# Two decoder layers: two weight blocks of a following stage split ahead into large buffers, and no weight remainders on GpSimd beside a norm

## The chip, the core and the metric

One core of a Trainium2 chip runs the whole program. The metric is device time of one execution in microseconds. A kernel's time is the median of its runs; the profile is one further execution, recorded instruction by instruction. PE is TensorE, DVE VectorE, ACT ScalarE, POOL GpSimd, and SP the engine that issues nearly all of the DMAs.

## The reference

512 tokens of width 1024 pass two layers. Layer 0 mixes tokens with multi-head latent attention, layer 1 with a sparse attention whose indexer picks keys per token. Each layer then cross-attends with 4 heads into 256 memory tokens and applies a SwiGLU FFN of hidden width 2816. Every sub-layer ends in a scaled residual and a layer norm:

```python
for i in range(DEPTH):
    y = mla_mixer(...) if i % 2 == 0 else dsa_mixer(...)
    x = layer_norm(ALPHA * x + y, ln_g[i, 0], ln_b[i, 0])
    y = memory_cross_attention(x, mem, xa_w_q[i], xa_w_kv[i], xa_w_o[i])
    x = layer_norm(ALPHA * x + y, ln_g[i, 1], ln_b[i, 1])
    y = swiglu_ffn(x, ffn_w_in[i], ffn_w_down[i])
    x = layer_norm(ALPHA * x + y, ln_g[i, 2], ln_b[i, 2])
```

## The kernel before

Everything is fp32, but TensorE multiplies in a rounded form (fp32r). So each operand is split into a high part, a cast on ACT (L103), and a low part, the remainder, a subtraction on DVE or, where the caller asks for it, on POOL (L105). A product is three matmuls, high by high, high by low, low by high (`mm3`, L126 to L129).

Weights come in blocks of 128x1024 (512 KB). `chunk` (L114) loads one with a DMA on SP's queue into `raw`, of which there are three buffers, and splits it into `wh` and `wl`, five buffers each. Activations live in a pool of 9 larger buffers (`t8`, 8 KB per partition): the residual stream x (2), its transposed split copies XT (4), a norm's coefficients gb (1), and the down-projection weights of the FFN with their sums and differences (`sp_weights`). A scheduler puts each engine's instructions in order by the program's order and by what they wait for, and gives each tile a buffer that is free; each engine then works through its list strictly in order.

The end of a sub-layer works on four tiles tt of 128 tokens. `out_proj_tm` (L407) multiplies the tokens of a tile with the output weights in two halves n of 512 columns, four k steps each. DVE adds each half to the residual (L367) and takes its statistics (L316). `Norm.affine` then merges the statistics (L324), adds the epsilon (L286), takes the power -1/2 on POOL, on one column (L288), and normalizes each half in two operations on DVE (L343, L345). `Norm.turn` transposes the eight 128x128 squares of the normalized tile on PE (L355) and splits them into XT, a cast from PSUM on ACT and a remainder on DVE. These steps are interleaved: affine(tt-1) comes behind the first half of tile tt, turn(tt-2) behind its k=1. The first tile ran k-major: for each k both halves n. So its n=0 was finished as the seventh of eight products.

Behind the second norm of each layer comes the first FFN group (`ffn`). It needs the four blocks (jj, gu) = (0,0), (0,1), (1,0), (1,1) of `ffn_in`; a pair gu = 0, 1 is a gate and its linear partner. Their products are taken in halves of 256 tokens, first all four blocks for tokens 0 to 255, with turn(2) and turn(3) of the norm behind the products of the first and the third, then all four for tokens 256 to 511. The blocks with jj + gu = 1 had their remainders on POOL.

Behind the third norm of layer 0 the sparse-attention layer begins with the value/indexer weights w_vi, 328 columns by 8 k steps, in three blocks of k 0 to 3, 3 to 6 and 6 to 8. The remainder of the middle one was on POOL. The products of token tile tt need all three blocks.

In cross-attention (`cross`), the query blocks of head hd+1 are loaded and multiplied while head hd is at work; then come that head's two key blocks `xa_k`. Head 3's queries are the last reader of XT in `cross`.

Of the kernel before, what the change touches and what calls it, by code (L numbers as in the profile page):

```python
# [11 lines left out]
F32 = mybir.dt.float32  # L12
# [8 lines left out]
P = 128  # L21
# [48 lines left out]
def tile_hybrid_mla_dsa_deepnorm_block(ctx: ExitStack, tc: tile.TileContext, A: dict, out: bass.AP):  # L70
# [42 lines left out]
    def chunk(src, shape, eng=None, after=(None, None)):  # L113
        n = int(np.prod(shape[1:]))  # L114
        raw = wp.tile([P, 1024], F32, tag="raw", name=nm("raw"), bufs=3)
        with behind(after[0]):
            load[0] = nc.sync.dma_start(raw[:, :n], src)
        h = wp.tile([P, 1024], FR, tag="wh", name=nm("wh"))
        l = wp.tile([P, 1024], FR, tag="wl", name=nm("wl"))
        split(h[:, :n], l[:, :n], raw[:, :n], eng, after[1])  # L120
        if len(shape) == 2:
            return h[:, :n], l[:, :n]
        k = shape[1]
        return (h[:, :n].rearrange("p (k m) -> p k m", k=k), l[:, :n].rearrange("p (k m) -> p k m", k=k))

    def mm3(ps, st, mv, start, stop, more=False):  # L126
        nc.tensor.matmul(ps, st[0], mv[0], start=start, stop=False, skip_group_check=more)  # L127
# [284 lines left out]
    def out_proj_tm(src, w, kc, norm):  # L412

        ws = [[chunk(w(n, c), (P, 2, 512)) for c in range(kc)] for n in range(2)]
        for tt in range(NT):
            ts_ = slice(P * tt, P * tt + P)

            def part(ps, n, k, c0, c1):
                sh, sl = src(k)
                wh, wl = ws[n][k // 2]  # L420
                return mm3(ps[:, c0:c1], (sh[:, ts_], sl[:, ts_]), (wh[:, k % 2, c0:c1], wl[:, k % 2, c0:c1]),
                           k == 0, k == 2 * kc - 1)

            first = [bank("b") for _ in range(2)] if tt == 0 else None
            if first:
                for k in range(2 * kc):
                    for n in range(2):
                        part(first[n], n, k, 0, 512)
            for n in range(2):
                parts = TAIL if n and norm.last and tt == NT - 1 else ((0, 512),)  # L430
                for c0, c1 in parts:
                    ps = first[n] if first else bank("b")
                    for k in range(0 if first else 2 * kc):
                        end = part(ps, n, k, c0, c1)
                        if tt > 1 and n == 0 and k == 1:
                            norm.turn(tt - 2, end)
                    if tt and n == 0:
                        norm.affine(tt - 1)
                    residual(ps, tt, n, False, c0, c1)
                    norm.stat(tt, n, c0, c1)  # L440
        norm.affine(NT - 1)
# [356 lines left out]

    def cross(i, XT, m, kv0):
        OT = []  # L800
        kvs = {0: kv0}
        pairs = []
        steps = iter(())

        def more(n):
            for _ in range(n):
                next(steps, None)

        def q_proj(hd):
            ws = [chunk(A["xa_q"][i, 2 * hd + dt], (P, NK, P)) for dt in range(2)]  # L810
            pq = proj_tiles(ws, XT, hd == 0)
            Q = []
            for dt in range(2):
                q = (t2(FR), t2(FR))
                split(q[0], q[1], pq[dt])
                Q.append(q)
            return Q

        def scores(hd, Q):
            Kt = kvs[hd][0]  # L820
            Sp = [t2(), t2()]
            sx = Softmax([Sp[qt // 2][:, 256 * (qt % 2):256 * (qt % 2) + 256] for qt in range(NT)])
            for qt in range(NT):
                ps = bank("b" if hd < 2 else "a")
                ts_ = slice(P * qt, P * qt + P)
                for dt in range(2):
                    mm3(ps[:, 0:256], (Q[dt][0][:, ts_], Q[dt][1][:, ts_]), (Kt[0][:, dt], Kt[1][:, dt]), dt == 0, dt == 1)
                sx.exp(qt, ps[:, 0:256], 1.0 / 16.0)
            return sx

        def turned(sx):
            Ss = sx.normalise()
            PT = []
            for mb in range(2):
                pt = bank("a")
                for qt in range(NT):
                    nc.tensor.transpose(pt[:, P * qt:P * qt + P], Ss[qt][:, P * mb:P * mb + P], ident)
                p_ = (t2(FR), t2(FR))
                split(p_[0], p_[1], pt)
                PT.append(p_)  # L840
            return PT

        def pv(hd, PT):
            Vt = kvs[hd // 2 * 2][1]
            eo = []
            for dt in range(2):
                po = bank("a")
                ds_ = slice(256 * (hd % 2) + P * dt, 256 * (hd % 2) + P * dt + P)
                for mb in range(2):
                    mm3(po, (Vt[mb][0][:, ds_], Vt[mb][1][:, ds_]), PT[mb], mb == 0, mb == 1)  # L850
                if hd < 2:
                    o = t2()
                    nc.scalar.copy(o, po)
                    eo.append(o)
                else:
                    o = (t2(FR), t2(FR))
                    split(o[0], o[1], po)
                    OT.append(o)
            if hd < 2:
                pairs.append(sp_operands(*eo))  # L860

        Q = q_proj(0)
        for hd in range(4):
            if hd == 1:
                W = sp_weights(A["xa_og"][i])
            Ss = scores(hd, Q)
            if hd < 3:
                more(1)
                Q = q_proj(hd + 1)
                more(2)  # L870
            else:
                more(3)
            PT = turned(Ss)
            if hd < 3:
                more(1)
                kvs[hd + 1] = xa_kv(i, hd + 1, m)
                more(1)
            else:
                more(3)
            pv(hd, PT)  # L880
            if hd == 1:
                steps = sp_steps(pairs, W, set())
                more(1)
            elif hd == 2:
                more(1)
        for _ in steps:
            pass
        return OT

    def sp_operands(e, o):  # L890

# [67 lines left out]
                radd(ps[t], t0 + t, n)  # L959
            yield  # L960

    def ffn(i, prev, norm_of, between=None):
        XT = prev.XT
        touched = set()
        steps = iter(())
# [12 lines left out]
        for gi, (j0, j1) in enumerate(FFN_GROUPS):  # L978
# [8 lines left out]
                WN = sp_weights(A["ffn_dg"][i, gi - 1])  # L987
            for j in range(j0, j1, 2):
                if j == 0:
                    ws = [chunk(A["ffn_in"][i, jj, gu], (P, NK, P), nc.gpsimd if jj + gu == 1 else None)  # L990
                          for jj in (j, j + 1) for gu in range(2)]
                    pss = proj_tiles(ws, XT, True, prev)
                    eo = [gate(pss[2 * jj], pss[2 * jj + 1]) for jj in range(2)]
                else:
                    eo = []
                    for jj in (j, j + 1):
                        pgu = []
                        for gu in range(2):
                            w = chunk(A["ffn_in"][i, jj, gu], (P, NK, P))
                            if first and gu:  # L1000
                                W.update(sp_weights(A["ffn_d0"][i], load[0]))
                                WN = sp_weights(A["ffn_dg"][i, 0])
                                first = False
                            if not first:
                                next(steps, None)
                            ps = bank("a")
                            proj(ps, w, XT, (0, 512))
                            if not first:
                                next(steps, None)
                            pgu.append(ps)  # L1010
                        eo.append(gate(*pgu))
                if not last:
                    pairs.append(sp_operands(*eo))
# [9 lines left out]
    out_proj(lambda k: OTs[k], lambda n, c: A["mla_o"][n, c], 4, norm, True)  # L1023
    mem = load_mem()
    kv0 = xa_kv(0, 0, mem)
    OT = cross(0, norm.XT, mem, kv0)
    norm = Norm(load_ln(0, 1))
    out_proj_tm(lambda k: OT[k], lambda n, c: A["xa_o"][0, n, c], 2, norm)
    norm = ffn(0, norm, lambda: Norm(load_ln(0, 2), spill=True), general_bias())
    r = nc.values_load(flag[0:1, 0:1], engines=(mybir.EngineType.SP,), min_val=0, max_val=1)  # L1030
    XT = norm.XT

# [7 lines left out]
    def stack_q_pool(ps, QA, QB):  # L1040
# [4 lines left out]
        nc.gpsimd.tensor_tensor(QA[64:128], f[0:64], QA[0:64].bitcast(F32), op=ALU.subtract)  # L1045
        nc.gpsimd.tensor_tensor(QB[0:64], f[64:128], QB[64:128].bitcast(F32), op=ALU.subtract)

    wvs = [chunk(A["w_vi"][:, NV * k0:NV * k1], (P, k1 - k0, NV), nc.gpsimd if k0 == 3 else None)
           for k0, k1 in ((0, 3), (3, 6), (6, 8))]
    VD = t8(FR, (P, 4, 4, P))  # L1050
    pk = bank("b")
    wi = cp.tile([P, NT, 8], F32, name="wi")
# [216 lines left out]
    out_proj(lambda k: OTd[k], lambda n, c: A["dsa_o"][n, c], 4, norm, True, pins)  # L1269
    mem = load_mem()  # L1270
    kv0 = xa_kv(1, 0, mem)
    OT = cross(1, norm.XT, mem, kv0)
    norm = Norm(load_ln(1, 1))
    out_proj_tm(lambda k: OT[k], lambda n, c: A["xa_o"][1, n, c], 2, norm)
    ffn(1, norm, lambda: Norm(load_ln(1, 2), last=True))

# [79 lines left out]
```

## Time and profile before

| | |
|---|---|
| median of 3 runs | 1520.51 us (1519.79 to 1521.77) |
| the profiled execution | 1521.89 us |
| its span, first to last instruction | 1520.0 us |
| granted TensorE clock, mean | 0.995 |

The page of the profile gives busy time by engine and a strip of 40 slices; groups of instructions are named by line and engine, with the time of one and the idle time ahead of it; a wait is named by the engine and the line that ended it. A row of a timeline has the start, the duration, the engine, the line, the operation, the output, the inputs and the count of merged instructions; where several are merged or follow without a gap, the durations overlap a little, so the distance of two starts is the better price of one. Stretches of time can be asked for with the busy time of every engine in each and the clock that PE was granted.

### The profile page before, as it was taken

What the parts mean: (1) busy time and instruction counts of PE and PEld (TensorE: products, weight loads), DVE (VectorE), ACT (ScalarE), POOL (GpSimd) and SP (SyncE); (2) the same over time, 40 slices, a digit from 0 to 9 for tenths busy, and PEclk for the clock granted to TensorE, in tenths of its full rate; (3) what the DMA queues carried; (4) which work ended last, traced back from release to release, by engine and by line L of the source; (5) the groups of instructions that cost most, each with busy time, mean ns of one, the idle gap of its engine ahead of it and who ended that gap; (6) DMA issues with size and microseconds to landing.
All of it is one profiled execution on the core that took longest, in us unless ns stands there. A gap on an engine that the chain in (4) does not pass through costs nothing. (4 is left out here: it accounts for less than half of the span.)

```text
span 1520.0 us, 20327 instructions
## 1 busy us (share of the span) xinstructions
PE 1481.5 (97%) x7600; PEld 1259.2 (83%) x7600; DVE 1073.5 (71%) x1818; ACT 670.2 (44%) x1196; POOL 374.9 (25%) x344
## 2 busy tenths in 40 slices
PE   9999999999999999999999989999999999999997
PEld 7788888988888888888888778898888888888886
DVE  7787869667857666565678989685678576566646
ACT  4677753444234333333256588344442433333331
POOL 1322003020223233150024653030103233142302
PEclk9999999999999999999999999999999999999999
DMA  6234423422332323222243146353323234223231
GB/s 216 72 103 111 149 82 128 154 82 83 99 110 98 125 71 125 90 95 93 91 153 102 53 161 227 111 167 98 104 77 111 70 99 137 85 96 125 71 97 56
DMA packets 50280, 166.16 MB, mean 109 GB/s; under 512 B 5188, under 2 KB 11732, under 8 KB 47364
## 3 DMA queue, kind: packets, MB, share of 16 engines
q1 hardware_dynamic: 49604, 163.61, 32.9%
q8 instruction: 60, 0.98, 0.3%
q10 hardware_dynamic: 576, 1.25, 0.2%
q14 instruction: 40, 0.33, 0.1%
HBM read 160.60 MB, written 9.47 MB: 112 GB/s over the span
## 5 line engine op out<-in xcount | busy, mean ns | idle before, releaser
L127 PE MATMUL ps<-t,wh 128*128 128x512 f32 (+2 forms) x1248 | 452.7, 363 | 6.0 <-DVE t L105 3.4
L128 PE MATMUL ps<-t,wh 128*128 128x512 f32 (+2 forms) x1248 | 450.5, 361 | 1.2 <-DVE t L105 1.2
L129 PE MATMUL ps<-t,wl 128*128 128x512 f32 (+2 forms) x1248 | 450.7, 361 | 0.0
L103 ACT CAST wh<-raw 128x1024 fp32r<-128x1024 f32 (+2 forms) x205 | 213.8, 1043 | 335.3 <-PE ps L128 148.3
L105 DVE TENSOR_TENSOR wl<-raw,wh 128x1024 fp32r<-128x1024 f32 (+3 forms) x179 | 246.6, 1380 | 123.1 <-ACT wh L103 122.1
L127 PE MATMUL ps<-wh,t 128*128 128x512 f32 (+3 forms) x760 | 289.5, 381 | 0.6 <-ACT wh L103 0.6
L128 PE MATMUL ps<-wl,t 128*128 128x512 f32 (+3 forms) x760 | 288.0, 379 | 1.9 <-DVE wl L105 1.9
L129 PE MATMUL ps<-wh,t 128*128 128x512 f32 (+3 forms) x760 | 287.7, 379 | 0.5 <-DVE t L105 0.4
L127 PEld LDWEIGHTS ps<-t,wh 128*128 128x128 f32 x1248 | 236.0, 189 | 44.0 <-DVE t L105 5.5
L128 PEld LDWEIGHTS ps<-t,wh 128*128 128x128 f32 x1248 | 236.2, 189 | 36.0 <-DVE t L105 1.5
L129 PEld LDWEIGHTS ps<-t,wl 128*128 128x128 f32 x1248 | 236.1, 189 | 35.1
L103 ACT CAST t<-ps 128x512 fp32r<-128x512 f32 (+2 forms) x241 | 118.2, 523 | 126.1 <-PE ps L355 86.7
L103 ACT CAST wh<-t 128x1024 fp32r<-128x1024 f32 (+1 forms) x84 | 82.3, 980 | 204.4 <-PE ps L128 172.2
L128 PEld LDWEIGHTS ps<-wl,t 128*128 128x128 f32 x760 | 143.6, 189 | 27.1 <-DVE wl L105 2.4
L129 PEld LDWEIGHTS ps<-wh,t 128*128 128x128 f32 x760 | 143.4, 189 | 26.5 <-DVE t L105 1.0
L127 PEld LDWEIGHTS ps<-wh,t 128*128 128x128 f32 x760 | 143.5, 189 | 25.4 <-ACT wh L103 0.8
L105 DVE TENSOR_TENSOR wl<-t,wh 128x1024 fp32r<-128x1024 f32 (+1 forms) x84 | 101.5, 1208 | 84.0 <-ACT wh L103 82.5
L105 DVE TENSOR_TENSOR t<-ps,t 128x512 fp32r<-128x512 f32 (+2 forms) x241 | 138.3, 603 | 13.9 <-ACT t L103 11.8
L288 POOL TENSOR_TENSOR sm<-sm,mhalf 128x1 f32<-128x1 f32 x32 | 30.4, 950 | 415.2 <-DVE sm L286 415.2
L105 DVE TENSOR_TENSOR t<-t,t 128x512 fp32r<-128x512 f32 (+3 forms) x133 | 102.8, 778 | 36.7 <-ACT t L103 34.0
L103 ACT CAST t<-t 128x512 fp32r<-128x512 f32 (+3 forms) x133 | 75.3, 572 | 84.9 <-POOL t L899 51.6
L970 DVE TENSOR_TENSOR t<-ps,t 128x512 f32<-128x512 f32 x44 | 30.4, 692 | 108.5 <-PE ps L129 108.5
(182 smaller groups left out, 1767.8 us busy)
## 6 DMA issues: line engine op xcount, KB each, us to landing
raw<-in_ffn_in_dram SPq DMA_DIRECT2D x88, 512.0 KB, 3.5
t<-in_ffn_dg_dram SPq DMA_DIRECT2D x16, 1024.0 KB, 5.1
raw<-in_xa_k_dram SPq DMA_DIRECT2D x16, 512.0 KB, 3.6
raw<-in_xa_v_dram SPq DMA_DIRECT2D x16, 512.0 KB, 4.6
raw<-in_xa_q_dram SPq DMA_DIRECT2D x16, 512.0 KB, 3.6
scr<-vscr SPq DMA_DIRECT2D x16, 319.5 KB, 4.3
raw<-in_w_uq_dram SPq DMA_DIRECT2D x8, 512.0 KB, 3.8
raw<-in_mla_o_dram SPq DMA_DIRECT2D x8, 512.0 KB, 4.2
```

Source lines behind the costliest of these rows:

```text
L103: nc.scalar.copy(h, src)
L105: low[0] = (eng or nc.vector).tensor_tensor(l, src, h.bitcast(F32), op=ALU.subtract)
L127: nc.tensor.matmul(ps, st[0], mv[0], start=start, stop=False, skip_group_check=more)
L128: nc.tensor.matmul(ps, st[0], mv[1], start=False, stop=False, skip_group_check=more)
L129: return nc.tensor.matmul(ps, st[1], mv[0], start=False, stop=stop, skip_group_check=more)
L288: nc.gpsimd.tensor_tensor(b, a, mhalf, op=ALU.pow)
L970: nc.vector.tensor_tensor(sg, pu, sg, op=ALU.mult)
```

## The change

It has three parts.

First, `chunk_ahead`. It loads a block through `raw` like `chunk`, but splits it into one large `t8` buffer, high part and remainder side by side, both on ACT and DVE. In `cross`, behind the queries of head 3, it takes the first two blocks (0,0) and (0,1) of the FFN's input; in the last group of layer 0's FFN, behind the first product of its last gate pair, it takes the first two blocks of w_vi.

Second, the blocks (1,0) and (1,1) and the third one of w_vi, still loaded by `chunk` in their old places, have their remainders on DVE. No remainder in these three places is on POOL any more: two in each FFN, one at w_vi.

Third, the first tile of `out_proj_tm` takes its eight products in another order, so that n=0 is finished as the fifth.

```diff
+    def chunk_ahead(src, k):
+        n = src.shape[-1]
+        raw = wp.tile([P, 1024], F32, tag="raw", name=nm("raw"), bufs=3)
+        nc.sync.dma_start(raw[:, :n], src)
+        t = t8(FR, (P, 2, 1024))
+        h, l = t[:, 0, :n], t[:, 1, :n]
+        split(h, l, raw[:, :n])
+        return [x.rearrange("p (k m) -> p k m", k=k) for x in (h, l)]
...
             if first:
-                for k in range(2 * kc):
-                    for n in range(2):
-                        part(first[n], n, k, 0, 512)
+                for n, k in ((0, 0), (0, 1), (0, 2), (1, 0), (0, 3), (1, 1), (1, 2), (1, 3)):
+                    part(first[n], n, k, 0, 512)
...
                 Q = q_proj(hd + 1)
+                if hd == 2:
+                    ahead += [chunk_ahead(A["ffn_in"][i, 0, gu], NK) for gu in range(2)]
...
                 if j == 0:
-                    ws = [chunk(A["ffn_in"][i, jj, gu], (P, NK, P), nc.gpsimd if jj + gu == 1 else None)
-                          for jj in (j, j + 1) for gu in range(2)]
+                    ws = ahead + [chunk(A["ffn_in"][i, j + 1, gu], (P, NK, P)) for gu in range(2)]
...
                             pgu.append(ps)
+                            if tail and (jj, gu) == (NJ - 1, 0):
+                                ahead += tail()
...
-    norm = ffn(0, norm, lambda: Norm(load_ln(0, 2), spill=True), general_bias())
+    norm = ffn(0, norm, ahead, lambda: Norm(load_ln(0, 2), spill=True), general_bias(),
+               lambda: [chunk_ahead(A["w_vi"][:, NV * k0:NV * k1], k1 - k0) for k0, k1 in ((0, 3), (3, 6))])
...
-    wvs = [chunk(A["w_vi"][:, NV * k0:NV * k1], (P, k1 - k0, NV), nc.gpsimd if k0 == 3 else None)
-           for k0, k1 in ((0, 3), (3, 6), (6, 8))]
+    wvs = ahead[-2:] + [chunk(A["w_vi"][:, 6 * NV:8 * NV], (P, 2, NV))]
```

What this moves, engine by engine; the lines of the changed kernel stand nine to twelve later (L288 is its L297, L316 its L325, L324 its L333, L286 its L295, L343 its L352, L345 its L354, L367 its L376, L923 to L925 its L934 to L936). POOL from the second norm of layer 0 to the first combination of down-projection weights, before; `sm` are the norm's one-column statistics, numbers tell tiles apart:

```order
L288 TENSOR_TENSOR sm_4267<-sm_4265,mhalf 128x1
L288 TENSOR_TENSOR sm_4322<-sm_4320,mhalf 128x1
L105 TENSOR_TENSOR wl_4420<-raw_4417,wh_4419 128x1024
L288 TENSOR_TENSOR sm_4377<-sm_4375,mhalf 128x1
L105 TENSOR_TENSOR wl_4426<-raw_4423,wh_4425 128x1024
L288 TENSOR_TENSOR sm_4405<-sm_4403,mhalf 128x1
L923 TENSOR_TENSOR t_1061_4742<-t_1060_4741 128x512
```

The same place in the changed kernel:

```order
L297 TENSOR_TENSOR sm_4277<-sm_4275,mhalf 128x1
L297 TENSOR_TENSOR sm_4332<-sm_4330,mhalf 128x1
L297 TENSOR_TENSOR sm_4387<-sm_4385,mhalf 128x1
L297 TENSOR_TENSOR sm_4415<-sm_4413,mhalf 128x1
L934 TENSOR_TENSOR t_1059_4740<-t_1058_4739 128x512
```

The two remainders between the powers of tiles 1 to 3 are gone from POOL's list. DVE at the norm of tile 3 in the same window, before; t_659 is the half of x that holds tiles 2 and 3, t_970 the coefficients, and the rows from `ps` are remainders of transposed tiles:

```order
L345 SCALAR_TENSOR_TENSOR t_659_2510<-t_659_2510,sm_4377,t_970_4188 128x512
L316 BN_STATS sm_4384<-t_659_2510 128x6
L367 TENSOR_TENSOR t_659_2510<-t_659_2510,ps_4386 128x512
L105 TENSOR_TENSOR wl_4432<-raw_4429,wh_4431 128x1024
L316 BN_STATS sm_4384<-t_659_2510 128x6
L105 TENSOR_TENSOR t_972_4192<-ps_4463,t_971_4191 128x4x128
L324 BN_AGGR sm_4401<-sm_4384 128x2
L105 TENSOR_TENSOR t_974_4194<-ps_4470,t_973_4193 128x4x128
L286 TENSOR_SCALAR sm_4403<-sm_4401 128x1
L343 SCALAR_TENSOR_TENSOR t_659_2510<-t_659_2510,sm_4401,t_970_4188 128x512 x2
L345 SCALAR_TENSOR_TENSOR t_659_2510<-t_659_2510,sm_4405,t_970_4188 128x512 x2
L105 TENSOR_TENSOR wl_4707<-raw_4704,wh_4706 128x1024
```

In the changed kernel:

```order
L354 SCALAR_TENSOR_TENSOR t_659_2510<-t_659_2510,sm_4387,t_974_4198 128x512
L325 BN_STATS sm_4394<-t_659_2510 128x6
L376 TENSOR_TENSOR t_659_2510<-t_659_2510,ps_4396 128x512
L105 TENSOR_TENSOR wl_4430<-raw_4427,wh_4429 128x1024
L325 BN_STATS sm_4394<-t_659_2510 128x6
L105 TENSOR_TENSOR wl_4705<-raw_4702,wh_4704 128x1024
L333 BN_AGGR sm_4411<-sm_4394 128x2
L105 TENSOR_TENSOR t_976_4202<-ps_4461,t_975_4201 128x4x128
L295 TENSOR_SCALAR sm_4413<-sm_4411 128x1
L352 SCALAR_TENSOR_TENSOR t_659_2510<-t_659_2510,sm_4411,t_974_4198 128x512 x2
L354 SCALAR_TENSOR_TENSOR t_659_2510<-t_659_2510,sm_4415,t_974_4198 128x512 x2
```

The remainder of block (2,0), which stood behind the norm of tile 3 (the last row before), now stands ahead of its L324; one of the two remainders of tile 2's transposes has gone behind the norm. SP's queue at head 3 of the cross-attention, before:

```order
L117 DMA raw_3814<-in_xa_q_dram 128x1024
L117 DMA raw_3926<-in_xa_k_dram 128x1024
L117 DMA raw_3956<-in_xa_k_dram 128x1024
L117 DMA raw_4195<-in_xa_o_dram 128x1024
L117 DMA raw_4201<-in_xa_o_dram 128x1024
```

In the changed kernel, where L129 is the DMA of `chunk_ahead`:

```order
L117 DMA raw_3814<-in_xa_q_dram 128x1024
L129 DMA raw_3878<-in_ffn_in_dram 128x1024
L129 DMA raw_3883<-in_ffn_in_dram 128x1024
L117 DMA raw_3936<-in_xa_k_dram 128x1024
L117 DMA raw_3966<-in_xa_k_dram 128x1024
L117 DMA raw_4205<-in_xa_o_dram 128x1024
```

The two ahead loads stand in front of the key blocks, and hold two of the three staging buffers there.

More of the change, by code (lines that the diff above doesn't have):

```diff
@@ L800, in cross @@
         OT = []
+        ahead = []
         kvs = {0: kv0}
@@ L887, in cross @@
             pass
-        return OT
+        return OT, ahead
     def sp_operands(e, o):
@@ L960, in sp_steps, with ffn @@
             yield
-    def ffn(i, prev, norm_of, between=None):
+    def ffn(i, prev, ahead, norm_of, between=None, tail=None):
         XT = prev.XT
@@ L1025, in tile_hybrid_mla_dsa_deepnorm_block @@
     kv0 = xa_kv(0, 0, mem)
-    OT = cross(0, norm.XT, mem, kv0)
+    OT, ahead = cross(0, norm.XT, mem, kv0)
     norm = Norm(load_ln(0, 1))
     out_proj_tm(lambda k: OT[k], lambda n, c: A["xa_o"][0, n, c], 2, norm)
-    norm = ffn(0, norm, lambda: Norm(load_ln(0, 2), spill=True), general_bias())
+    norm = ffn(0, norm, ahead, lambda: Norm(load_ln(0, 2), spill=True), general_bias(),
+               lambda: [chunk_ahead(A["w_vi"][:, NV * k0:NV * k1], k1 - k0) for k0, k1 in ((0, 3), (3, 6))])
     r = nc.values_load(flag[0:1, 0:1], engines=(mybir.EngineType.SP,), min_val=0, max_val=1)
@@ L1271, in tile_hybrid_mla_dsa_deepnorm_block @@
     kv0 = xa_kv(1, 0, mem)
-    OT = cross(1, norm.XT, mem, kv0)
+    OT, ahead = cross(1, norm.XT, mem, kv0)
     norm = Norm(load_ln(1, 1))
     out_proj_tm(lambda k: OT[k], lambda n, c: A["xa_o"][1, n, c], 2, norm)
-    ffn(1, norm, lambda: Norm(load_ln(1, 2), last=True))
+    ffn(1, norm, ahead, lambda: Norm(load_ln(1, 2), last=True))
 def _fm(w):
```

## The prediction

> **What bounds the kernel now.** I read the page first, then the waits of TensorE, then its rows around the longest of them, then VectorE and GpSimd at the same moments. The page gives TensorE nearly the whole span:
>
> ```profile
> PE 1481.5 (97%) x7600; PEld 1259.2 (83%) x7600; DVE 1073.5 (71%) x1818; ACT 670.2 (44%) x1196; POOL 374.9 (25%) x344
> ```
>
> So time can only be won where TensorE stands still, 1520.0 - 1481.5 = 38.5 us in all, or where it runs at less than its full clock. The table of waits (total, times, longest) puts one reason at the head:
>
> ```profile
> PE ps L355 <- DVE t L345: 6.2, 6, 1.3
> ```
>
> L355 is the transpose of a normalized token tile, L345 the second half of that normalization on VectorE. The six waits are three in each layer, where the second norm (after cross-attention) runs into the first FFN group. TensorE's timeline in the first layer (start, duration, group, in brackets idle time and releaser):
>
> ```profile
> 404.81 1.04 PE L355 MATMUL ps<-ident,t 128*128 128x128 f32 x8
> 405.60 0.47 PE L127 MATMUL ps<-wh,t 128*128 128x512 f32 x1
> ...
> 412.68 0.60 PE L355 MATMUL ps<-ident,t 128*128 128x128 f32 x4
> 414.53 0.63 PE L355 MATMUL ps<-ident,t 128*128 128x128 f32 x4 [1.25 <-DVE t L345]
> ...
> 420.63 0.28 PE L129 MATMUL ps<-t,wl 128*128 128x256 f32 x1
> ...
> 423.80 0.36 PE L127 MATMUL ps<-t,wh 128*128 128x256 f32 x1
> ...
> 425.32 0.28 PE L127 MATMUL ps<-t,wh 128*128 128x256 f32 x1
> ```
>
> The eight transposes of tile 1 run unhindered and cost 405.60 - 404.81 = 0.79 us from start to start. Those of tile 2 break in the middle: 414.53 - 412.68 = 1.85, where half of 0.79 would do, so 1.45 is lost. Between the last product before tile 3's transposes and the first behind them lie 3.17 us; 0.12 (one product's spacing) and 0.79 would do, so 2.26 is lost. Window 1 (about 404 to 425): **3.71 us**.
>
> The second layer has the same window:
>
> ```profile
> 1159.10 0.60 PE L355 MATMUL ps<-ident,t 128*128 128x128 f32 x4
> 1160.99 0.63 PE L355 MATMUL ps<-ident,t 128*128 128x128 f32 x4 [1.29 <-DVE t L345]
> ...
> 1167.10 0.28 PE L129 MATMUL ps<-t,wl 128*128 128x256 f32 x1
> ...
> 1173.27 0.28 PE L127 MATMUL ps<-t,wh 128*128 128x256 f32 x1
> ```
>
> Tile 2 loses 1.89 - 0.40 = 1.49. For tile 3 I compare like with like: 1167.10 and 1173.27 are the same two products as 420.63 and 425.32; here 6.17 us lie between them, there 4.69, so the loss is 2.26 + 1.48 = 3.74. Window 3: **5.23 us**. The extra 1.48 is clock, as the table of stretches shows (length, busy time and count of PE, PEld, DVE, ACT, POOL, then granted clock, DMA share, GB/s):
>
> ```profile
> 386.00:424.00 38.00, 34.93 (x203) 30.33 (x202) 34.48 (x50) 9.06 (x12) 12.84 (x9) 1.00 0.26 86
> 700.00:742.00 42.00, 42.00 (x187) 34.78 (x186) 20.89 (x24) 13.09 (x16) 0.00 (x0) 1.00 0.31 97
> 1168.00:1172.00 4.00, 2.80 (x14) 2.57 (x15) 4.00 (x4) 1.18 (x2) 2.84 (x2) 0.72 0.30 57
> 1172.00:1176.00 4.00, 4.00 (x31) 4.00 (x30) 1.21 (x3) 0.00 (x0) 0.00 (x0) 0.85 0.85 335
> ```
>
> Right behind window 3's stalls the granted clock is 0.72 and 0.85; window 1 stays at 1.00 with the same stalls.
>
> Window 2 is the start of the sparse-attention layer, where the remainder of the third value/indexer weight block comes late:
>
> ```profile
> 770.50 0.41 PE L128 MATMUL ps<-wl,t 128*128 128x328 f32 x1 [1.53 <-DVE wl L105]
> ```
>
> 1.53 idle, and by the ratio of 1.45 lost to 1.25 idle above some 0.2 for the restart: **1.7 us**.
>
> Why VectorE is late: in 386 to 424 it works 34.48 of 38 us, and part of that work is stretched. VectorE and GpSimd, window 1:
>
> ```profile
> 406.36 2.77 DVE L343 SCALAR_TENSOR_TENSOR t<-t,sm,t 128x512 f32<-128x512 f32 x1
> ...
> 410.26 2.20 DVE L345 SCALAR_TENSOR_TENSOR t<-t,sm,t 128x512 f32<-128x512 f32 x1
> ...
> 413.65 0.74 DVE L345 SCALAR_TENSOR_TENSOR t<-t,sm,t 128x512 f32<-128x512 f32 x1
> 414.31 0.68 DVE L316 BATCH_NORM_STATS2 sm<-t 128x6 f32<-128x512 f32 x1
> 414.91 0.66 DVE L367 TENSOR_TENSOR t<-t,ps 128x512 f32<-128x512 f32 x1
> 415.50 1.21 DVE L105 TENSOR_TENSOR wl<-raw,wh 128x1024 fp32r<-128x1024 f32 x1
> 416.64 0.68 DVE L316 BATCH_NORM_STATS2 sm<-t 128x6 f32<-128x512 f32 x1
> 417.24 0.67 DVE L105 TENSOR_TENSOR t<-ps,t 128x512 fp32r<-128x512 f32 x1
> 417.83 0.19 DVE L324 BATCH_NORM_AGGREGATE sm<-sm 128x2 f32<-128x12 f32 x1
> 417.95 0.63 DVE L105 TENSOR_TENSOR t<-ps,t 128x512 fp32r<-128x512 f32 x1
> 418.50 0.13 DVE L286 TENSOR_SCALAR sm<-sm 128x1 f32<-128x1 f32 x1
> 418.56 1.40 DVE L343 SCALAR_TENSOR_TENSOR t<-t,sm,t 128x512 f32<-128x512 f32 x2
> 419.88 3.45 DVE L345 SCALAR_TENSOR_TENSOR t<-t,sm,t 128x512 f32<-128x512 f32 x2
> ```
>
> ```profile
> 406.18 2.41 POOL L105 TENSOR_TENSOR wl<-raw,wh 128x1024 fp32r<-128x1024 f32 x1 [5.45 <-ACT wh L103]
> ...
> 409.52 2.40 POOL L105 TENSOR_TENSOR wl<-raw,wh 128x1024 fp32r<-128x1024 f32 x1
> ...
> 419.68 1.42 POOL L923 TENSOR_TENSOR t<-t 128x512 f32<-128x512 f32 x1
> ```
>
> An affine half costs 0.74 where GpSimd is quiet (0.66 from start to start), but 2.77 and 2.20 beside GpSimd's two weight remainders; each ends about 0.54 behind GpSimd's, as if it had done its work only then: 406.36 + 2.77 = 409.13 against 408.59, and 412.46 against 411.92. Operations that read PSUM (L367, the L105 of t<-ps) show no such thing. The last pair costs 3.45 instead of 1.40 beside the first combination of down-projection weights on GpSimd (L923).
>
> **The change part by part.**
>
> *Remainders off GpSimd, window 1.* The stretched halves return 2.77 - 0.74 = 2.03 and 2.20 - 0.74 = 1.46, 3.49 us ahead of tile 2's last L345. The first tile's new order finishes column half n=0 two products earlier, so its residual add and statistics run while n=1 is still being multiplied. Ahead of L324 stand two L367 and two L316 of 0.6 each: before, all four count from the seventh product, now the last two count from the eighth. A product is three matmuls of 512 columns, an estimated 3 x 0.24 = 0.7 by the 0.12 of 256 columns, so tile 0's L324, and the unbroken list behind it, comes 2.4 - 0.7 - 1.2 = 0.5 to 0.6 earlier. Tile 2 is normalized at 413.65 + 0.66 - 3.49 - 0.6 = 410.2; TensorE asks for its second half at 412.68 + 0.40 = 413.1. The stall of 1.45 goes, with 2.9 us to spare.
>
> *Tile 3.* From 410.2 VectorE does, by the starts in the rows above, L316 0.60, L367 0.59, the remainder of block (1,1) 1.14, L316 0.60, then a remainder that stood behind the norm before (block (2,0), 1.14 more), L324 0.12, one t<-ps remainder 0.6, L286 0.06, L343 1.32 for both halves, L345 0.66 each: 417.7. TensorE comes to the second half of tile 3's transposes at 420.63 + 0.12 - 1.45 + 0.40 = 419.7. Slack 2.0 us, so the 2.26 goes too. The weights that L923 combines arrive later in the changed program (their load waits for the norm's coefficient buffer, which is free only behind this L345), so L923 lands behind the norm, where VectorE has its slack.
>
> *Ahead loads.* Two 1.05 us casts and two 1.2 us remainders per layer move to head 3 of cross-attention. The holes there, on ScalarE and on VectorE, and the load that pays:
>
> ```profile
> 353.96 1.05 ACT L103 CAST wh<-t 128x1024 fp32r<-128x1024 f32 x1 [3.90 <-PE ps L128]
> ```
>
> ```profile
> 346.13 1.22 DVE L105 TENSOR_TENSOR wl<-raw,wh 128x1024 fp32r<-128x1024 f32 x1
> ...
> 355.04 1.23 DVE L105 TENSOR_TENSOR wl<-t,wh 128x1024 fp32r<-128x1024 f32 x1 [3.61 <-ACT wh L103]
> ```
>
> ```profile
> raw<-in_xa_k_dram SPq DMA_DIRECT2D x16, 512.0 KB, 3.6
> ```
>
> ```profile
> 360.46 0.28 PE L127 MATMUL ps<-t,wh 128*128 128x256 f32 x1
> ```
>
> 2.1 of 3.90 and 2.4 of 3.61 us are taken. On SP's queue the two loads go in front of head 3's key blocks, and with three staging buffers the second key block's load now waits for the first one's remainder, which ends at 346.13 + 1.22 = 347.35. It lands 3.6 later near 351.0, is cast by 352.1 and split by 353.3; TensorE wants it at 360.46. Slack 7 us, cost nothing. The ahead tiles take the old activations' buffers, free when head 3's query product is done with them, which is what ScalarE's cast at 353.96 waited for behind its hole (its releaser is TensorE's L128); the loads of the output projection go out some 7 us later, behind the ahead splits, and are wanted only at the out-projection, whose third tile TensorE is at when row 404.81 comes.
>
> *Window 2.* The two early blocks are split in the last FFN group (row 700:742: TensorE full, VectorE busy 20.89 of 42, ScalarE 13.09), which adds 2.3 and 2.1 us there, covered. The affine half there that ran beside the middle block's remainder on GpSimd:
>
> ```profile
> 762.08 2.65 DVE L343 SCALAR_TENSOR_TENSOR t<-t,sm,t 128x512 f32<-128x512 f32 x1
> ```
>
> The remainder that row 770.50 waits for stood behind most of this stretched work in VectorE's order. It now stands ahead of tile 0's norm, and the half at 762.08 shrinks by 1.9. Bounds: 1.53 (idle alone) to 2.0 (a small later stop also gone); taken 1.7.
>
> *Window 3* is window 1 again: 1.49 + 2.26 = 3.75 for sure, and 1.48 of cold clock. In this profile it follows the stall; of two like windows one has it, so a run may have none, one or two of them. [...]
>
> **Sum.** 3.71 + 1.7 + 5.23 = 10.6 for a run with one dip: the profiled run of 1521.89 would come to 1511.3. The median of before, 1520.51, lies 1.38 lower, perhaps without that dip; then 3.71 + 1.7 + 3.75 = 9.2 is due. I take the middle, 9.9: 1520.51 - 9.9 = **1510.6**. Own range of this case, both dips or none: 1508.4 to 1512.
>
> **Rivals.**
>
> *Tile 3 stays late.* If the extra 1.14 us ahead of L324, plus 0.9 us of anything else (a GpSimd rsqrt queued late, a slow cast), uses up the 2.0 us, the stalls at tile 3 come back in part in both layers. For it: tile 3 had 2.26 of lateness in before, VectorE is busy 34.48 of the 38 us to 424. Against it: no L923 beside L345 now. At most 2.26 twice: 9.2 - 4.5 = 4.7 left, so 1513 to 1516, at 0.2.
>
> *Nothing gained.* The five remainders, 1.2 us each on VectorE, just replace the stretching: needs that the 2.77 and 2.20 had another cause than GpSimd. Against it: of the affine rows quoted, long are exactly those beside a GpSimd operation of 1.4 us or more. 1518 to 1522, at 0.08.
>
> *Window 2's gain lost* in the sparse-attention stage, where TensorE waits for VectorE's selection anyway: 1512.3; inside the first case's price, at 0.06.
>
> *Slower.* Place: SP's queue at head 3. If the second key block, or the buffers of the old activations, come more than 7 us late, ScalarE and VectorE stand in order behind the ahead split, and TensorE starves in both layers; it needs (9.9 + 3)/2 = 6.5 us each beyond the slack, thus a block 13 us late, to end at 1523.5 or above. Landing at 3.6 speaks against it: at 0.04.
>
> **Chances.** Forecast 0.62, tile 3 0.2, window 2 0.06, nothing 0.08, slower 0.04. Within 0.2% (3.0 us, about what a measurement of this kernel can tell from no change) lies "nothing"; faster 0.88, same 0.08, slower 0.04. Range 1508.0 to 1516: it holds the forecast, window 2 and most of tile 3.
>
> **What would show it.** Right: the L355 rows on L345 vanish from the waits; no affine half over 0.8 us in the two windows; TensorE's w_vi products run unbroken; head 3 without a gap on TensorE; clock 1.00 behind window 3. Wrong: L355 waiting still at tile 3, TensorE idle between 345 and 364, or the affine halves still at 2 us with GpSimd quiet.

## The result, and the profile after

The changed kernel takes 1509.11 us (median of 4 runs, 1508.10 to 1512.59) beside 1520.9 of the kernel before (4 runs, 1519.79 to 1521.77): ratio 0.9927, 95% interval 0.9909 to 0.9945, 11.8 us by the medians. 1510.6 was forecast. The profiled execution has 1508.1 us and a span of 1506.2, 13.8 less than the one of before.

The page after, and three stretches that hold the three windows (columns as before):

```profile
PE 1476.6 (98%) x7600; PEld 1256.1 (83%) x7600; DVE 1064.8 (71%) x1823; ACT 669.8 (44%) x1196; POOL 362.6 (24%) x339
```

```profile
330.00:386.00 56.00, 56.00 (x301) 48.27 (x300) 43.78 (x72) 29.38 (x50) 5.92 (x5) 1.00 0.32 104
386.00:422.00 36.00, 36.00 (x226) 32.41 (x226) 31.46 (x53) 8.59 (x13) 3.96 (x4) 1.00 0.27 88
...
742.00:780.00 38.00, 38.00 (x225) 34.94 (x224) 32.11 (x59) 12.47 (x22) 6.34 (x5) 1.00 0.32 111
...
1124.00:1163.00 39.00, 39.00 (x244) 35.05 (x243) 32.90 (x54) 10.32 (x14) 3.96 (x4) 1.00 0.25 82
```

In all three windows TensorE is now busy for the whole stretch, at full clock, and in the stretch at head 3 of cross-attention (330 to 386) it still is. The wait of the transposes is gone from the table of waits, whose first row is now the one that stood second before:

```profile
PE ps L136 <- DVE t L105: 3.4, 4, 1.2
```

The transposes of tiles 1, 2 and 3 in window 1 run in one piece each:

```profile
402.60 1.04 PE L364 MATMUL ps<-ident,t 128*128 128x128 f32 x8
410.47 1.04 PE L364 MATMUL ps<-ident,t 128*128 128x128 f32 x8
417.09 1.04 PE L364 MATMUL ps<-ident,t 128*128 128x128 f32 x8
```

VectorE and GpSimd there, tiles 2 and 3:

```profile
403.93 0.74 DVE L352 SCALAR_TENSOR_TENSOR t<-t,sm,t 128x512 f32<-128x512 f32 x1
...
405.79 0.74 DVE L354 SCALAR_TENSOR_TENSOR t<-t,sm,t 128x512 f32<-128x512 f32 x1
...
407.71 0.74 DVE L354 SCALAR_TENSOR_TENSOR t<-t,sm,t 128x512 f32<-128x512 f32 x1
...
413.16 1.40 DVE L352 SCALAR_TENSOR_TENSOR t<-t,sm,t 128x512 f32<-128x512 f32 x2
414.48 1.41 DVE L354 SCALAR_TENSOR_TENSOR t<-t,sm,t 128x512 f32<-128x512 f32 x2
```

```profile
404.10 0.99 POOL L297 TENSOR_TENSOR sm<-sm,mhalf 128x1 f32<-128x1 f32 x1 [5.80 <-DVE sm L295]
413.32 0.99 POOL L297 TENSOR_TENSOR sm<-sm,mhalf 128x1 f32<-128x1 f32 x1 [8.24 <-DVE sm L295]
424.01 1.30 POOL L934 TENSOR_TENSOR t<-t 128x512 f32<-128x512 f32 x1 [9.70 <-PE ps L138]
```

No affine half is longer than 0.75. GpSimd has only the norm's powers there, and the first combination of down-projection weights starts at 424.01, 8 us behind the last half.

To see where the time came from, the same products of TensorE are set side by side. Four of them in the profile of before (the first, 404.81, stands in the prediction):

```profile
432.52 0.28 PE L127 MATMUL ps<-t,wh 128*128 128x256 f32 x1
...
783.25 0.31 PE L127 MATMUL ps<-wh,t 128*128 128x328 f32 x1
...
1151.28 1.03 PE L355 MATMUL ps<-ident,t 128*128 128x128 f32 x8
...
1180.45 0.28 PE L127 MATMUL ps<-t,wh 128*128 128x256 f32 x1
```

and after:

```profile
426.59 0.28 PE L136 MATMUL ps<-t,wh 128*128 128x256 f32 x1
...
775.12 0.31 PE L136 MATMUL ps<-wh,t 128*128 128x328 f32 x1
...
1142.65 1.04 PE L364 MATMUL ps<-ident,t 128*128 128x128 f32 x8
...
1166.65 0.28 PE L136 MATMUL ps<-t,wh 128*128 128x256 f32 x1
```

The lead of the changed kernel, by how much earlier the same product starts, is 2.21 us ahead of window 1, 5.93 behind it, 8.13 behind window 2, 8.63 ahead of window 3 and 13.80 behind it. So window 1 gave 3.72, window 2 gave 2.20, the sparse-attention layer between 0.50 (its cause was not sought), window 3 gave 5.17: 11.6 us. The first 2.21 have nothing to do with the change: 0.5 lies ahead of TensorE's first products, and the rest is a stretch of low clock in the first attention, which of these two profiles only the one of before has (last section).

### The profile page after: what moved, and what is told of

The parts are those of the page before. It is cut to its first block, busy times and chain, and to the rows that moved or that the text cites. A ratio compares the mean times of both kernels' runs of the same rounds, so it can differ in the third digit from the quotient of the medians.

```text
span 1506.2 us, 20338 instructions
## 1 busy us (share of the span) xinstructions
PE 1476.6 (98%) x7600; PEld 1256.1 (83%) x7600; DVE 1064.8 (71%) x1823; ACT 669.8 (44%) x1196; POOL 362.6 (24%) x339
## 5 line engine op out<-in xcount | busy, mean ns | idle before, releaser
L136 PE MATMUL ps<-t,wh 128*128 128x512 f32 (+2 forms) x1184 | 433.9, 367 | 6.0 <-DVE t L105 3.4
L137 PE MATMUL ps<-t,wh 128*128 128x512 f32 (+2 forms) x1184 | 432.0, 365 | 1.2 <-DVE t L105 1.2
L138 PE MATMUL ps<-t,wl 128*128 128x512 f32 (+2 forms) x1184 | 432.0, 365 | 0.0
L103 ACT CAST wh<-raw 128x1024 fp32r<-128x1024 f32 (+1 forms) x199 | 207.6, 1044 | 318.3 <-PE ps L137 133.9
L105 DVE TENSOR_TENSOR wl<-raw,wh 128x1024 fp32r<-128x1024 f32 (+3 forms) x178 | 242.9, 1367 | 111.0 <-ACT wh L103 110.0
L136 PE MATMUL ps<-wh,t 128*128 128x512 f32 (+2 forms) x736 | 281.3, 382 | 0.1
L138 PE MATMUL ps<-wh,t 128*128 128x512 f32 (+2 forms) x736 | 279.6, 380 | 0.4 <-DVE t L105 0.4
L137 PE MATMUL ps<-wl,t 128*128 128x512 f32 (+2 forms) x736 | 279.6, 380 | 0.4 <-DVE wl L105 0.4
L136 PEld LDWEIGHTS ps<-t,wh 128*128 128x128 f32 x1184 | 223.2, 189 | 43.6 <-DVE t L105 5.5
L137 PEld LDWEIGHTS ps<-t,wh 128*128 128x128 f32 x1184 | 223.4, 189 | 36.2 <-DVE t L105 1.5
L138 PEld LDWEIGHTS ps<-t,wl 128*128 128x128 f32 x1184 | 223.3, 189 | 35.1
L138 PEld LDWEIGHTS ps<-wh,t 128*128 128x128 f32 x736 | 138.3, 188 | 26.1 <-DVE t L105 0.7
L137 PEld LDWEIGHTS ps<-wl,t 128*128 128x128 f32 x736 | 138.4, 188 | 25.3 <-DVE wl L105 0.6
L136 PEld LDWEIGHTS ps<-wh,t 128*128 128x128 f32 x736 | 138.4, 188 | 24.8 <-ACT wh L103 0.4
L297 POOL TENSOR_TENSOR sm<-sm,mhalf 128x1 f32<-128x1 f32 x32 | 30.4, 951 | 435.0 <-DVE sm L295 435.0
```

What stands on the lines that cost most here:

```text
L103: nc.scalar.copy(h, src)
L105: low[0] = (eng or nc.vector).tensor_tensor(l, src, h.bitcast(F32), op=ALU.subtract)
L137: nc.tensor.matmul(ps, st[0], mv[1], start=False, stop=False, skip_group_check=more)
L138: return nc.tensor.matmul(ps, st[1], mv[0], start=False, stop=stop, skip_group_check=more)
L297: nc.gpsimd.tensor_tensor(b, a, mhalf, op=ALU.pow)
```

## The experiments

The theory to test (A): GpSimd's weight remainders hold up VectorE's affine halves, and taking them away is what pays. The rivals: VectorE was late from its load, so that the blocks split ahead pay (B); or the norm's power, queued on GpSimd behind a remainder, was what VectorE waited for (C).

**Only the remainders moved.** The kernel before with this, and the like at w_vi:

```diff
-ws = [chunk(A["ffn_in"][i, jj, gu], (P, NK, P), nc.gpsimd if jj + gu == 1 else None)
+ws = [chunk(A["ffn_in"][i, jj, gu], (P, NK, P))
```

> The kernel before with one edit: the five weight remainders beside the norms (two in each first FFN group, one at w_vi) on VectorE instead of GpSimd; nothing loaded ahead, the first tile in its old order. Theory A (a GpSimd operation that reads SBUF holds up VectorE's operations with two SBUF inputs until it is over): the 2.77 and 2.20 us affine halves shrink to 0.74, two remainders of 1.14 are added; tile 2 is ready at about 411.9, before TensorE asks at 412.7, so its 1.45 us stall goes; tile 3 stays some 1.7 to 2.0 late, because the first combination of down-projection weights still runs beside its last pair. About 1.9 us gained in windows 1 and 3 each and 0.8 in window 2: 4.6 in all, 1516.3 us (1.5 less or more with a cold-clock stretch). Rival B (VectorE is late from sheer load, the long halves have another cause): 2.3 us more load per window and no shorter halves, so slower by 4 to 5 us, about 1525.

Measured: 1510.58 us beside 1521.63, ratio 0.9931 (0.9917 to 0.9944). That is nearly the whole gain, over twice what was expected, with 2.3 us more work in VectorE's list per FFN window. B falls. What was expected wrongly is tile 3. Its last pair on VectorE, the first combination on GpSimd, and TensorE's wait in window 2:

```profile
414.34 1.40 DVE L343 SCALAR_TENSOR_TENSOR t<-t,sm,t 128x512 f32<-128x512 f32 x2
415.66 1.41 DVE L345 SCALAR_TENSOR_TENSOR t<-t,sm,t 128x512 f32<-128x512 f32 x2
```

```profile
418.16 1.80 POOL L923 TENSOR_TENSOR t<-t 128x512 f32<-128x512 f32 x1 [2.67 <-DMA t<-in_ffn_d_dram]
```

```profile
768.97 0.42 PE L129 MATMUL ps<-wh,t 128*128 128x328 f32 x1 [0.98 <-DVE t L105]
```

In the kernel before, L923 ran beside tile 3's late pair. Here it starts when its weights land. Freed of the two stretches, the pair is over at 416.98, before L923 starts; the collision that cost 3.45 - 1.40 = 2.05 us before does not take place. TensorE's transposes of tile 3 start at 416.97 and run in one piece, so this version has next to no slack there. One wait is left, 0.98 us in window 2.

**Only the new order of the first tile.**

```diff
-for k in range(2 * kc):
-    for n in range(2):
-        part(first[n], n, k, 0, 512)
+for n, k in ((0, 0), (0, 1), (0, 2), (1, 0), (0, 3), (1, 1), (1, 2), (1, 3)):
+    part(first[n], n, k, 0, 512)
```

> The kernel before with only the new order of the first tile's eight products. Both theories: the unbroken list of VectorE starts 0.5 to 0.6 us earlier in the three windows, worth at most 0.6 each: 1.2 to 1.8 us, 1519.4. Under A the shift also changes which affine half meets a GpSimd remainder, so single halves may be long in other places; under B nothing else changes.

Measured: 1523.64 us beside 1521.63, ratio 1.0021 (1.0011 to 1.0032), slower and not faster. The halves did move against the remainders, and not for the better (GpSimd, then VectorE):

```profile
404.22 2.96 POOL L105 TENSOR_TENSOR wl<-raw,wh 128x1024 fp32r<-128x1024 f32 x1 [5.69 <-ACT wh L103]
407.14 0.55 POOL L288 TENSOR_TENSOR sm<-sm,mhalf 128x1 f32<-128x1 f32 x1
407.65 2.40 POOL L105 TENSOR_TENSOR wl<-raw,wh 128x1024 fp32r<-128x1024 f32 x1
```

```profile
404.17 0.74 DVE L343 SCALAR_TENSOR_TENSOR t<-t,sm,t 128x512 f32<-128x512 f32 x1
404.82 1.28 DVE L105 TENSOR_TENSOR t<-ps,t 128x512 fp32r<-128x512 f32 x2
407.72 2.88 DVE L345 SCALAR_TENSOR_TENSOR t<-t,sm,t 128x512 f32<-128x512 f32 x1 [1.61 <-POOL sm L288]
```

L343 now starts 0.05 ahead of GpSimd's remainder, and this time it is the remainder that is long, 2.96 instead of 2.40. The tile's power stands in GpSimd's queue behind it, so that VectorE is idle for 1.61 us, and then the next remainder holds L345 for 2.88. The pair between them, which reads PSUM, is not stretched: 1.28 us beside the remainder, 1.27 to 1.28 elsewhere. The six waits of the transposes come to 7.3 us instead of 6.2, and the wait in window 2 to 1.84 instead of 1.53. So C exists too, as a companion: in the kernel before it was covered by the stretched half.

**The change without the new order**, and **the change with both remainders of the second pair, blocks (1,0) and (1,1), on GpSimd** (in the kernel before, those of (0,1) and (1,0) were there):

```diff
-ws = ahead + [chunk(A["ffn_in"][i, j + 1, gu], (P, NK, P)) for gu in range(2)]
+ws = ahead + [chunk(A["ffn_in"][i, j + 1, gu], (P, NK, P), nc.gpsimd) for gu in range(2)]
```

> The changed kernel with the first tile in its old order. By the profile of the change tile 2 was ready at 408.4 and tile 3 at 415.8, 2.4 and 1.7 us ahead of TensorE, so 0.6 us later costs nothing: the change's own time within 0.5 us, 1509.1, no waits of the transposes on the second affine operation. If the order carried weight, 1 to 2 us more.

> The changed kernel with the remainders of blocks (1,0) and (1,1) on GpSimd again in both layers. Theory A: the first of the two runs ahead of the norm and harms nothing, the second runs 2.4 us somewhere beside tile 1's or tile 2's affine halves and stretches one or two of them by 1 to 2 us each, but VectorE is spared 2.3 us of remainders, and tile 2 and 3 have 2.4 and 1.7 us to spare: a wait of at most 0.5 us per window, 1509 to 1510.5. Rival C (any remainder on GpSimd beside the norm brings the stalls back): 2 to 4 us per window, 1513 to 1517.

Measured: 1510.5 (ratio 0.9925, 0.9911 to 0.9938) and 1510.16 (0.9932, 0.9918 to 0.9945), neither with a wait in the three windows. The first ratio is the change's own, 0.9927, within the interval. So the order carries nothing that shows here, and two remainders on GpSimd can be borne if the rest leaves room. Where the second one fell, in window 1:

```profile
403.82 2.94 POOL L105 TENSOR_TENSOR wl<-raw,wh 128x1024 fp32r<-128x1024 f32 x1 [5.70 <-ACT wh L103]
```

```profile
407.30 0.75 DVE L354 SCALAR_TENSOR_TENSOR t<-t,sm,t 128x512 f32<-128x512 f32 x1 [1.61 <-POOL sm L297]
```

```profile
416.91 1.22 PE L364 MATMUL ps<-ident,t 128*128 128x128 f32 x8
```

It cost VectorE 1.61 us by the queue, not the stretch that was expected, and the slack took it, with none left at tile 3: its transposes (last row) take 1.22 us instead of 1.04. The experiment tells that a remainder there hurts only without slack; it does not tell A from C.

**Only the two FFN blocks ahead.** The kernel before with `chunk_ahead` in `cross` alone, the remainder of block (1,0) on GpSimd, w_vi as before, old order.

> The kernel before with only the two FFN blocks loaded ahead: the remainder of block (1,0) stays on GpSimd, w_vi stays as it was, the first tile in its old order. The remainder on GpSimd now runs ahead of the norm, where it meets no affine half. So windows 1 and 3 should be free of waits (9.0 us by the profile of the change, its cold-clock stretch included, 7.5 without), and window 2 keeps its 2.2: 1511.5 to 1513. If the halves on GpSimd were needed in VectorE's list for the gain, some wait stays at tile 3 and it is 1514 to 1517.

Measured: 1512.71 us beside 1520.8, ratio 0.9941 (0.9927 to 0.9954). Windows 1 and 3 are free of waits, window 2 has kept its own:

```profile
387.04 2.38 POOL L105 TENSOR_TENSOR wl<-raw,wh 128x1024 fp32r<-128x1024 f32 x1 [45.81 <-ACT wh L103]
```

```profile
PE ps L137 <- DVE wl L105: 1.5, 1, 1.5
```

The remainder of block (1,0) is still on GpSimd, but runs at 387, ahead of the norm; that of (0,1) is done on VectorE at head 3. So each of the two parts alone clears windows 1 and 3: one takes the remainders off GpSimd, the other takes them out of the norm's time.

**Doses on the changed kernel.** With VectorE's list unchanged, work is added to GpSimd in the second norm: behind each tile's power two subtractions of a scratch tile (reads and writes), or two memsets (writes only), or ahead of it two more powers.

```diff
+if self.dose:
+    with behind(low[0]):
+        for _ in range(2):
+            nc.gpsimd.tensor_tensor(dz, dz, dz, op=ALU.subtract)   # or memset(dz, 0.0)
```

> The changed kernel with two more GpSimd subtractions of 128x512 on a scratch tile (read and written) behind each power of the second norm's four tiles, in both layers; VectorE's list is the same. They leave the result alone. Theory A (a GpSimd operation that reads SBUF holds up VectorE's operations with two SBUF inputs until it is over): at some 1.3 us each they hold an affine half of every tile by 1.9 to 2.4 us, 8 to 9 us along VectorE's list, of which 1.8 to 2.9 is slack: the waits of the transposes return with some 5 to 7 us per window, 1519 to 1524 us. Rival B (sheer load of VectorE, GpSimd does not matter): 1509 to 1510, no affine half over 0.8.

> The same with two memsets of the scratch tile in place of the two subtractions: GpSimd is as occupied by work that writes SBUF and reads none. If the hold is one of reads, no affine half is longer than 0.8 and the time is the change's, 1509 to 1510.5. If any work of GpSimd on SBUF holds VectorE, the halves are stretched by the memsets' length, 1513 to 1522.

> The changed kernel with two more powers of one column (0.99 us each) on GpSimd ahead of the one that counts, for the four tiles of the second norm in both layers. This is the other way in which a remainder on GpSimd could hurt: the norm's power stands in its queue. The second affine operation waits some 1.2 to 1.9 us more per tile, 6 us along the list, less 1.8 to 2.5 of slack: 3 to 5 us per window, 1515 to 1519, with idle time of VectorE ended by the power and no half longer than 0.8. If one-column operations also hold VectorE's reads, the first affine operations would be long too.

Measured: subtractions 1517.83 us (0.998, 0.9966 to 0.9993), so over two thirds of the gain lost; memsets 1509.44 (0.9924, 0.9909 to 0.9939), nothing lost; powers 1512.05 (0.9942, 0.9927 to 0.9958), 2.6 us lost against the memsets. Subtractions, GpSimd and VectorE, and TensorE's waits in window 1:

```profile
393.85 2.63 POOL L341 TENSOR_TENSOR dz<-dz 128x512 f32<-128x512 f32 x2
```

```profile
394.05 2.98 DVE L361 SCALAR_TENSOR_TENSOR t<-t,sm,t 128x512 f32<-128x512 f32 x2
```

```profile
PE ps L371 <- DVE t L361: 2.7, 3, 1.0
```

Memsets:

```profile
393.39 1.11 POOL L341 MEMSET dz<- 128x512 f32 x2
```

```profile
393.61 1.41 DVE L361 SCALAR_TENSOR_TENSOR t<-t,sm,t 128x512 f32<-128x512 f32 x2
```

Powers:

```profile
391.25 1.66 POOL L298 TENSOR_TENSOR sm<-sm,mhalf 128x1 f32<-128x1 f32 x2 [52.01 <-DVE sm L295]
392.87 0.55 POOL L300 TENSOR_TENSOR sm<-sm,mhalf 128x1 f32<-128x1 f32 x1
```

```profile
391.09 1.41 DVE L356 SCALAR_TENSOR_TENSOR t<-t,sm,t 128x512 f32<-128x512 f32 x2
393.45 1.42 DVE L358 SCALAR_TENSOR_TENSOR t<-t,sm,t 128x512 f32<-128x512 f32 x2 [0.96 <-POOL sm L300]
```

The subtractions stretch the pair beside them from 1.41 to 2.98, and it ends 0.55 behind them (394.05 + 2.98 = 397.03 against 393.85 + 2.63 = 396.48), as the long halves of the kernel before did. The memsets, in the same place, leave the pair at 1.41, though they overlap it. The two kinds differ in length too (2.63 and 1.11 us a pair), so it is not the size of the loss that tells them apart but that no half beside a memset is stretched at all. The added powers stretch nothing either (1.41 beside 1.66 us of them); they hurt by the queue alone, 0.96 idle. Both losses fell short of what was expected (1519 to 1524 us with the subtractions, 1515 to 1519 with the powers): in window 1 the subtractions hold tiles 0 and 3 by 1.6 us each and tiles 1 and 2 by 0.9, 4.9 in all instead of 8 to 9, and the powers leave VectorE idle for 2.5 us in all instead of 6.

So an affine half, which reads two tiles in SBUF (`t<-t,sm,t`), is held by a GpSimd subtraction that reads SBUF (a pair takes 2.98 us instead of 1.41) and not by a memset, which only writes it (1.41). In the long halves quoted from before and in this pair GpSimd's operation had started first (406.18 against 406.36, 409.52 against 410.26, 393.85 against 394.05). With the order alone VectorE's L343 had started first (404.17 against 404.22), and there the remainder was the long one, 2.96 us instead of 2.40. The one-column powers, which read SBUF too, show no hold.

**A small version.** Remainders on VectorE and the early load of two w_vi blocks; no FFN blocks ahead, old order. It and the change ran twice, the second time on one chip:

> The first experiment's remainders on VectorE plus the early load of two w_vi blocks; no FFN blocks ahead, the first tile in its old order. If the remainders carry windows 1 and 3, and the early load the last 1 us of window 2, it equals the change: 1509 to 1510.5, no wait in any of the three windows. If the FFN blocks ahead count, 1 to 3 us slower than the change.

> The small version (remainders on VectorE, two w_vi blocks early, nothing else) once more, beside the change on the same chip. No wait in any of the three windows in either, so the same within 0.1%: 1508 to 1510. Should the work that the change puts into cross-attention cost something, the small version is 0.5 to 1 us faster.

> The change itself, for the comparison with the small version on one chip: 1508 to 1510.

Measured: 1508.11 (0.9916, 0.9902 to 0.9929), and then 1509.93 (0.9926, 0.9912 to 0.9939) beside 1509.38 (0.9923, 0.9909 to 0.9936) of the change. No wait in any of the three windows in either. They are the same within what can be told; no version here beats the change, but the small one does it with less.

## Why the prediction was right

- *What bounds, and by how much.* Window 1 was sized at 3.71 us and gave 3.72; window 3 at 5.23, its low clock included, and gave 5.17. Reading the loss from start to start, rather than from busy time (38.00 - 34.93 = 3.07 in window 1), was what made the size right.
- *Window 2* was the term that was sized too low: 1.7 taken from 1.53 to 2.0, and it gave 2.20. Part of it is a stop of 0.28 behind the wait, which had been put into the upper end only.
- *The median.* The middle between one stretch of low clock and none was taken, 9.9 us; the medians differ by 11.8 and the ratio says 11.1. The sum for a run with one such stretch, 10.6, was nearer. How many stretches a run has can't be foreseen from one profile, so about 1.5 us of the distance either way is luck. The upper end of the case's own range was added up wrongly: with no stretch it is 1520.51 - 9.2 = 1511.3, not 1512; the result lies inside either way.
- *Tiles 2 and 3.* Tile 2 was to be ready at 410.2 and tile 3 at 417.7; with the lead of 2.21 taken off, 408.0 and 415.5. The last halves end at 407.71 + 0.66 = 408.37 and 414.48 + 1.32 = 415.80. Their slack was put at 2.9 and 2.0 and is 410.47 + 0.40 - 408.37 = 2.5 and 417.09 + 0.40 - 415.80 = 1.7.
- *The first combination.* That it would land behind the norm was right, the reason only in part. Its load does go out later, at 415.92 instead of 412.32, right behind the last L354, and lands 4.8 us after that. But row 424.01 starts 3.3 us later still, released by a product of TensorE (`<-PE ps L138`).
- *Nothing lost at head 3.* The late key block's cast stands 1.5 us for its load, and TensorE is full from 330 to 386. Rival "slower" had no part.
- *The cause.* "As if it had done its work only then" is confirmed by the doses (the pair beside the subtractions ends 0.55 us behind them, the halves of before 0.54). But the prediction worked out the two parts only together, and the experiments show that either alone clears windows 1 and 3: they overlap. It also counted 0.5 to 0.6 us per window for the new order as part of the way; alone it is slower by 0.2%, and without it the change takes the same time. The rivals "tile 3 stays late" and "nothing gained" did not come about; the one-part kernel shows why the first was less likely than its 0.2, since lateness at tile 3 came mostly from a collision (2.05 of 2.26 us) that an earlier tile 3 escapes.

## What to carry to other kernels

Before work is given to GpSimd because VectorE is busy, look at what VectorE does beside it: a 2.4 us subtraction on GpSimd spared VectorE 1.14 us and held one of its halves for 2.03. By these runs such a helper belongs where VectorE's operations read PSUM (1.28 us beside a remainder, 1.27 to 1.28 elsewhere) or are not awaited (the remainder at 387 us, ahead of the norm), or it should only write (a pair of halves took 1.41 us beside two memsets, as without them). And a stall that one removal clears may be cleared by others as well: try the parts alone before all of them are kept.

## What the runs showed of the hardware

The low clock came in short stretches (0.57 to 0.85 over 4 us in those quoted here and in the prediction), seen in the profile of before at 1168 to 1176 us, in that of the order-only kernel in window 1, in 5 of the 13 profiles near 50 us in the first attention, and in all 13 in the sparse-attention layer at 872 to 893 us, in six of them twice as long. In the last two places all the kernels do the same work. Order only (columns as before), the profile of before near 50 us, and the profile after in the sparse-attention layer:

```profile
420.00:424.00 4.00, 2.61 (x15) 2.38 (x16) 3.72 (x5) 1.17 (x2) 3.04 (x2) 0.81 0.27 56
424.00:428.00 4.00, 4.00 (x29) 4.00 (x29) 0.15 (x1) 0.00 (x0) 0.00 (x0) 0.77 0.50 207
```

```profile
46.00:50.00 4.00, 2.02 (x9) 1.22 (x9) 3.67 (x7) 2.01 (x5) 1.60 (x2) 1.00 0.80 246
50.00:54.00 4.00, 4.00 (x23) 4.00 (x22) 2.09 (x4) 1.33 (x3) 2.75 (x2) 0.57 0.52 175
```

```profile
868.00:872.00 4.00, 2.39 (x18) 1.97 (x16) 3.90 (x18) 2.76 (x8) 3.77 (x6) 1.00 0.83 262
872.00:876.00 4.00, 3.77 (x17) 3.49 (x18) 3.43 (x21) 4.00 (x19) 0.17 (x1) 0.57 0.00 0
```

Each of these four comes in or right behind a few us in which TensorE stood idle for some 30 to 50% (2.80, 2.61, 2.02 and 2.39 busy of 4). That alone does not bring one: in the profile of before TensorE is busy for 2.18 of the 4 us from 420, and the clock stays at 1.00. Of the eight windows 1 and 3 in the four profiles in which their transposes wait (before, order only, subtractions, powers) two have such a stretch; of the eighteen in the nine profiles without those waits none; that points to the waits, and is too few to prove it. One costs about 1.5 us (1.48 in window 3, 1.7 near 50 us), and the clock goes with a good part of what the runs of one kernel differ by: of the 39 runs of the kernel before beside the experiments, the six with a mean clock of 0.997 have a median of 1518.5 us, the five with 0.994 one of 1522.6. In window 3 the waits are 0.81 to 1.29 us, with TensorE idle for 1.2 of the 4 us from 1168; the prediction counted the stretch there by that trace, 1.48 of its 5.23 us, and the result, 5.17, agreed.
